# The output projections of a two-layer decoder trunk: products, operands and the norm behind them in a written order on TensorE, VectorE and ScalarE

## The chip, the cores and the metric

The kernel runs on one core of a Trainium2 chip. TensorE multiplies matrices into PSUM banks, VectorE (DVE) and ScalarE (ACT) work elementwise on SBUF and PSUM, GpSimd (POOL) works elementwise on SBUF, SyncE (SP) issues transfers. The metric is the device time of one execution in microseconds (us). A measurement of this kernel tells differences of about 0.2% from no change.

## The reference

The reference is a causal decoder trunk of two layers on one sequence of 1024 tokens with 1024 features, in float32. Layer 0 is an RMSNorm, a sparse attention (compressed blocks, selected blocks and a sliding window), a residual, an RMSNorm, a SwiGLU block (FFN) with 2816 hidden features, and a residual. Layer 1 has dilated attention over shared keys and values, with three groups of heads merged, and then the same residual, norm and FFN. What matters here is the seam between attention and FFN, in both layers: the attention's rows times the output weights are added to x, and h = rmsnorm(x) goes into x + (silu(h W_gate) * (h W_up)) W_down, with

```python
def rmsnorm(x, g):
    x32 = x.astype(jnp.float32)
    y = x32 * lax.rsqrt(jnp.mean(x32 * x32, axis=-1, keepdims=True) + RMS_EPS)
    return (y * g.astype(jnp.float32)).astype(x.dtype)
```

## The kernel before, in words

**Precision.** A float32 operand of TensorE is split into a high part `ph` (ScalarE, L884) and a low part `pl`, the rest (VectorE, or GpSimd where `Pairs` is called with it, L885). A pair costs one instruction on each of the two engines. `mm3` multiplies two pairs with three matmuls of 128x512: high by high (L203), then L204 and L205 with one low part each. The norm's operands are split in the same way by `split` (L165 on ScalarE, L166 on VectorE).

**The output projection** `out_proj` multiplies the attention's rows (tile `oT` in layer 0, `oTb` in layer 1) by the output weights (tile `ow`) and adds the result to the residual rows `xr`. The 1024x1024x1024 product is cut into 512x512 blocks and done with seven block products, in this order: B11, B21, T1, T2, B22, T3, T4. Each has four chunks (k-slices of 128), and each chunk multiplies four row tiles `t` by 512 columns: 4 x 3 = 12 matmuls a chunk, 48 a block product, 336 in all. The left operands are blocks of the attention's rows (B11, B21, B22 and T4's) or sums of blocks, built by VectorE: L1213 adds two blocks for T1, L1214 subtracts for T2, L1215 for B22, L1216 for T3. The right operands are blocks of the weights; those whose names begin with T come precombined from memory, and their low parts are made by GpSimd. Results gather in two groups of four banks, `dx0` to `dx3` and `dr0, dr1, ux, uy`. After a block product the row-adds (L1204, one for each row tile) add the four banks to `xr` on VectorE. T3 and T4 both gather in the `dx` banks, T4 going on with T3's sums, so a product of T4 may write to a bank only when T3's row-add has read it. T4 takes its row tiles one after the other over all four chunks; the others go chunk by chunk.

**The norm behind it.** Rows 0 to 3 (of eight row tiles) are complete after B22. `B.half(xr, 0, ...)` norms them: a square with a sum over the first 512 columns (ScalarE, L1011) and one over the second 512 (VectorE, L1012), a sum of the two (L1014), a root (ScalarE, L1015), a reciprocal (L1016), a scaled copy of each half (VectorE L1017, ScalarE L1018) into eight tiles `xn`. TensorE then transposes them (L990), and they are split into the FFN's operands B11 and B21. Rows 4 to 7 get the same treatment later, within the FFN.

**Order.** A list of steps is run by `staged` (L901): each step's `prep` is issued ahead of the previous step's `run`, so the first chunk of a block product is prepared one step ahead, and within a step each chunk's operands are built just ahead of its products. The norm is a step of its own ahead of T4. This is the order in which the program is written; a scheduler that goes by estimated times then places the instructions of all engines, so products of the output projection may stand between instructions of the attention, and norm instructions between operands. The pair buffers are 6 deep, those with GpSimd's low parts 4.

**The neighbours.** In the FFN, `load_up` fetches up weights (SyncE, L1267) into places of `oT` that the output projection no longer needs, and GpSimd multiplies them by the norm's gains (L1269). `dense` calls all this once per layer. The dilated attention ahead of layer 1's projection ends with the merge of its groups (matmuls L1745, products on VectorE L1746, sums on GpSimd L1747).

Of the kernel before, what the change touches and what calls it, by code (L numbers as in the profile page):

```python
# [10 lines left out]
F32 = mybir.dt.float32  # L11
F32R = mybir.dt.float32r
BF = mybir.dt.bfloat16
AF = mybir.ActivationFunctionType
# [6 lines left out]
D = 1024  # L21
# [94 lines left out]
def trunk(ctx, tc, I, out):  # L116
# [278 lines left out]
    with ExitStack() as c:  # L395
# [153 lines left out]
        next(made)  # L549
        for _ in steps:  # L550
            pass
        kc2 = blocks_tile()
# [618 lines left out]
    def out_steps(spare, pairs, tmp, blocks, right, xr):  # L1171


        held = {}
        n = len(blocks)
        S_ = [tmp(i) for i in range(n)]

        def step(left, name, group, first, where, sums=None, whole=False):
            def operands(i):
                if sums is not None:  # L1180
                    sums(i, *blocks[i])
                return pairs(left(i)), right(name, i)

            def prep():
                ready = [operands(0)]

                def run():
                    if whole:
                        ready.extend(operands(i) for i in range(1, n))
                        order = [(i, t) for t in range(4) for i in range(n)]  # L1190
                    else:
                        order = [(i, t) for i in range(n) for t in range(4)]
                    if first:
                        held[group] = [bank((f"dx{t}", spare[t])[group]) for t in range(4)]
                    banks = held[group]
                    for i, t in order:
                        if i == len(ready):
                            ready.append(operands(i))
                        a, b = ready[i]
                        mm3(banks[t], part(a, t), b, first and i == 0, i == n - 1, True)  # L1200
                        if i == n - 1:
                            r, c = where
                            xs = xr[:, 4 * r + t, c * 512:(c + 1) * 512]
                            nc.vector.tensor_add(xs, xs, banks[t])  # L1204
                return run
            return prep

        A = lambda j: lambda i: blocks[i][j]
        T = lambda i: S_[i]
        sub, add = nc.vector.tensor_sub, nc.vector.tensor_add  # L1210
        return [step(A(0), "B11", 0, True, (0, 0)),
                step(A(2), "B21", 1, True, (0, 0)),
                step(T, "T1", 1, True, (1, 1), lambda i, a11, a21, a12, a22: add(S_[i], a21, a22)),  # L1213
                step(T, "T2", 0, False, (0, 1), lambda i, a11, a21, a12, a22: sub(S_[i], S_[i], a11)),  # L1214
                step(A(2), "B22", 1, False, (0, 1), lambda i, a11, a21, a12, a22: sub(a12, a12, S_[i])),  # L1215
                step(A(1), "T3", 0, False, (1, 1), lambda i, a11, a21, a12, a22: sub(a21, a11, a21)),  # L1216
                step(A(3), "T4", 0, False, (1, 0), whole=True)]

    def out_proj(layer, pw, pp, p, xr, oT, w, x_src, norm):
        pairs, made = Pairs(pp, 6), Pairs(p, 4)  # L1220
        raw = {}
# [8 lines left out]

        def right(name, i):
            t = raw[name, i]
            return pairs(t) if name[0] == "B" else made(t, nc.gpsimd)
# [163 lines left out]
    def dense(layer, w, x_src, oT, tail, near, far):  # L1397
# [3 lines left out]
        with ExitStack() as c:  # L1401
# [4 lines left out]
            with ExitStack() as c2:  # L1406
                pw, pp, p = [pool(c2, n, near) for n in ("fow", "fop", "fo")]
                out_proj(layer, pw, pp, p, xr, oT, w, x_src, B.half(xr, 0, ("dr0", "dr1", "ux", "uy"), places(p)))
# [430 lines left out]
```

## Time and profile before

| | us |
|---|---|
| median of three runs | 2977.77 |
| lowest, highest | 2974.25, 2978.2 |
| the profiled execution's own time | 2971.67 |
| its span in the trace | 2969.9 |
| output projection, layer 0: last attention matmul, first FFN product | 724.66, 815.92 |

In rows of the profile, `PE dx L203 <- DVE nss L1016` means that a matmul of line 203 into tile dx waited, and that the last thing it waited for was VectorE's instruction of line 1016 on tile nss. A wait is put down to the engine's instruction that was counted last, so the instruction that matters can stand right behind the one named. Windows give the busy time of each engine within a stretch, the number of instructions, and the clock that TensorE was granted (1.00 is full). At full clock the products of the output projection follow each other by 0.2267 us.

### The profile page before, as it was taken

The page shows a single profiled execution, that of the slowest core. Times are in us where ns is not written, and L with a number is a line of the kernel's source. Part 1 is how long each engine was busy: PE and PEld are TensorE (multiplying, and loading weights), DVE is VectorE, ACT ScalarE, POOL GpSimd, SP SyncE. Part 2 cuts the span into 40 slices and gives each one's busy share as a digit, 9 for nine tenths or more (in the row PEclk, how much of TensorE's full clock was granted, in tenths as well). Part 3 has the DMA queues.
Part 4 walks back from the last instruction along what each step waited for, and adds up shares of the span by engine and source line. Part 5 has one row for each costly group of instructions (what it writes and reads, how often), then busy time and mean ns, then how long its engine had stood idle before and what let it go on. Part 6 is the DMA issues. An engine that isn't in the chain of part 4 may idle for free.

```text
span 2969.9 us, 44462 instructions
## 1 busy us (share of the span) xinstructions
PE 2839.8 (96%) x14734; PEld 2368.8 (80%) x14734; DVE 2398.1 (81%) x4875; ACT 1608.9 (54%) x3614; POOL 1607.7 (54%) x1718
## 2 busy tenths in 40 slices
PE   9999999999999999999999999899989999999997
PEld 8888888887777788788777788788867787887885
DVE  5553988988888888988876676699998888888887
ACT  5432888897553333333454444799965433333334
POOL 3135766764565555555557786444426655556551
PEclk9999999999999999999999999999999999999998
DMA  8678133113222222231224555966340211112112
GB/s 252 209 246 285 46 91 87 54 30 118 68 62 64 73 75 62 62 81 53 86 81 143 160 165 152 288 195 181 101 167 22 68 57 53 57 47 64 54 43 75
DMA packets 277318, 317.58 MB, mean 107 GB/s; under 512 B 19196, under 2 KB 210733, under 8 KB 277088
## 3 DMA queue, kind: packets, MB, share of 16 engines
q1 hardware_dynamic: 255344, 246.50, 27.9%
q0 software_dynamic: 21744, 68.23, 7.1%
q8 instruction: 117, 1.92, 0.3%
q14 instruction: 113, 0.93, 0.1%
HBM read 243.17 MB, written 87.20 MB: 111 GB/s over the span
## 4 chain that ended last, share of the span: by engine, by line
PE 62%; DVE 23%; ACT 6%; issue 4%; POOL 2%; DMA 2%; SPq 1%; DVEq 0%; ACTq 0%; POOLq 0%
PE ux L203 5%; PE ux L204 5%; DVE pl L885 5%; PE ux L205 5%; PE uy L203 4%; PE uy L204 4%; PE uy L205 4%; DVE xr L943 4%; PE dx L204 3%; PE dx L205 3%; PE pt L328 3%; PE dr L203 3%; PE dx L203 3%; PE mm L204 3%; PE mm L203 3%
## 5 line engine op out<-in xcount | busy, mean ns | idle before, releaser
L885 DVE TENSOR_TENSOR pl<-oT,ph 128x512 fp32r<-128x512 f32 x319 | 327.2, 1045 | 42.5 <-ACT ph L884 37.2
L884 ACT ACTIVATE ph<-oT 128x512 fp32r<-128x512 f32 x329 | 198.4, 625 | 206.8 <-PE ux L204 58.9
L328 PE MATMUL pt<-ident,P 128*128 128x128 f32 x1536 | 242.3, 275 | 10.6 <-DVE tl L166 4.9
L885 DVE TENSOR_TENSOR pl<-oTb,ph 128x512 fp32r<-128x512 f32 x233 | 222.3, 979 | 25.2 <-ACT ph L884 25.2
L166 DVE TENSOR_TENSOR tl<-pt,th 128x512 fp32r<-128x512 f32 (+1 forms) x336 | 217.4, 652 | 26.8 <-ACT th L165 25.5
L884 ACT ACTIVATE ph<-oTb 128x512 fp32r<-128x512 f32 x239 | 142.8, 625 | 170.2 <-PE ux L204 52.5
L943 DVE TENSOR_TENSOR xr<-xr,dr 128x512 f32<-128x512 f32 x320 | 204.3, 678 | 29.9 <-PE dr L205 29.9
L204 PE MATMUL dx<-pl,ph 128*128 128x512 f32 x512 | 206.3, 403 | 9.9 <-DVE pl L885 7.3
L803 POOL TENSOR_SCALAR P<-P,sm,gates 128x384 f32<-128x384 f32 (+7 forms) x256 | 182.5, 724 | 45.2 <-DVE sm L801 40.0
L165 ACT ACTIVATE th<-pt 128x512 fp32r<-128x512 f32 (+1 forms) x336 | 185.0, 564 | 37.4 <-PE pt L328 31.6
L205 PE MATMUL dx<-ph,pl 128*128 128x512 f32 x512 | 202.5, 398 | 0.3 <-DVE pl L885 0.3
L328 PEld LDWEIGHTS pt<-ident,P 128*128 128x128 f32 x1536 | 177.7, 141 | 31.4 <-DVE tl L166 5.2
L943 DVE TENSOR_TENSOR xr<-xr,dx 128x512 f32<-128x512 f32 x320 | 199.9, 676 | 2.5 <-PE dx L205 1.8
L203 PE MATMUL dx<-ph 128*128 128x512 f32 x512 | 165.6, 403 | 15.9 <-DVE nss L1016 7.9
L799 ACT ACTIVATE P<-P,m 128x384 f32<-128x384 f32 (+7 forms) x256 | 170.6, 669 | 9.0 <-DVE m L797 7.2
L1269 POOL TENSOR_TENSOR oT<-oT,gffn 128x512 f32<-128x512 f32 x92 | 107.7, 1177 | 118.8 <-DMA oT<-in_ffn_w_up_dram 96.5
L348 PE MATMUL o<-th,V 128*128 128x256 f32 x572 | 158.7, 297 | 4.5 <-DVE o L360 1.7
L349 PE MATMUL o<-tl,V 128*128 128x256 f32 x572 | 158.2, 299 | 4.7 <-DVE tl L166 1.7
L1269 POOL TENSOR_TENSOR oTb<-oTb,gffn 128x512 f32<-128x512 f32 x92 | 106.5, 1167 | 87.9 <-DMA oTb<-in_ffn_w_up_dram 79.8
L341 POOL TENSOR_SCALAR th<-traw 128x256 fp32r<-128x256 f32 x112 | 95.4, 852 | 98.2 <-ACT traw L340 33.1
L1646 ACT ACTIVATE P<-P,st 128x384 f32<-128x384 f32 (+2 forms) x256 | 139.9, 548 | 6.3 <-DVE st L1641 5.0
L203 PEld LDWEIGHTS dx<-ph 128*128 128x128 f32 x512 | 97.8, 191 | 45.4 <-ACT nss L1015 8.7
(629 smaller groups left out, 9487.8 us busy)
## 6 DMA issues: line engine op xcount, KB each, us to landing
qB<-xr POOLq DMA_DIRECT2D x96, 256.0 KB, 4.6
oT<-in_ffn_w_up_dram SPq DMA_DIRECT2D x92, 256.0 KB, 3.0
oTb<-in_ffn_w_up_dram SPq DMA_DIRECT2D x92, 256.0 KB, 3.0
Q<-qB SPq DMA_DIRECT2D x40, 512.0 KB, 6.4
wd<-in_ffn_w_down_dram SPq DMA_DIRECT2D x66, 256.0 KB, 2.6
oT<-in_b_w_q_dram SPq DMA_DIRECT2D x48, 256.0 KB, 3.4
K<-kBs SPq DMA_DIRECT2D x40, 256.0 KB, 9.6
wraw<-in_a_w_in_dram SPq DMA_DIRECT2D x18, 512.0 KB, 7.1
```

The source lines that it names most:

```text
L165: prev = nc.scalar.activation(H_, src, AF.Copy)
L166: rest = (eng or nc.vector).tensor_sub(L_, src, f32(H_))
L203: nc.tensor.matmul(ps, lh, rh, start=first, stop=False, skip_group_check=bool(shared))
L204: nc.tensor.matmul(ps, lh, rl, start=False, stop=False, skip_group_check=bool(shared))
L205: return nc.tensor.matmul(ps, ll, rh, start=False, stop=last, skip_group_check=bool(shared))
L328: nc.tensor.transpose(ps[:, i * 128:(i + 1) * 128], b, ident)
L799: nc.scalar.activation(P[:, e, :n], P[:, e, :n], AF.Exp, bias=mm[:, e:e + 1], scale=-1.0, accum_out=sm[:, e:e + 1])
L803: nc.gpsimd.tensor_scalar(P[:, e, :n], P[:, e, :n], sm[:, e:e + 1], gt(g, t, br, 2 * hp + e, 1), op0=OP.mult, op1=OP.mult)
L884: nc.scalar.activation(h, src, AF.Copy)
L885: (eng or nc.vector).tensor_sub(l, src, f32(h))
L943: nc.vector.tensor_add(xs, xs, banks[t])
L1269: nc.gpsimd.tensor_mul(v, v, gains[:, k:k + 4].unsqueeze(2).to_broadcast([128, 4, 128]))
```

## The change

In `out_proj` the list of steps is gone (`out_steps` is deleted), and the seven block products stand in a loop within `tc.manual_schedule` for TensorE, VectorE and ScalarE: what is written there keeps its order on these three engines. Instructions of other parts can still be put between them by the scheduler; GpSimd and SyncE stay with the scheduler.

- Operands are built two chunks ahead of their products; GpSimd's right operands are asked for two chunks further ahead (`right(n + 2)` in `operands(n)`). The pair buffers are 8 deep (before 6), GpSimd's 5 (before 4).
- In each chunk all three matmuls of a row tile are written together, tile by tile.
- The norm of rows 0 to 3 is written into the last two block products. While T3 runs, behind the operands of each chunk, `squares(i)` takes one square of 1024 columns on ScalarE with its sum (line 1244 of the new program) and the root (1245); `scaled(i - 1)` then takes the reciprocal (1250) and the scaled copy, on VectorE alone for odd tiles (1252, 1024 columns) and half by half on VectorE and ScalarE for even ones (1254, 1255). The sums L1014 and the squares L1012 of this half are gone. The `xn` tiles are four of 1024 columns.
- T4 runs tile by tile; the transposes into B11 come behind its first tile, those into B21 behind the third.
- In layer 0's attention one step of the output of blocks (`next(made)`) moves behind the rest of the compression's steps.

New line numbers: the left sums are 1206 to 1209, the row-adds 1236, the FFN's gain products 1310, the merge's matmuls 1786. What a name with a number means below: `nss2_` a tile's sum of squares, `ph_`/`pl_` one pair's parts, `ow_` a right block, `xn` a normed tile.

First place, ScalarE in layer 0 from the norm's roots to the last operands of T4. Before:

```order
L884 ACTIVATE ph_10912<-ow_10270 128x512
L1015 ACT_TABLE_LOAD
L1015 ACTIVATE nss2_10733<-nss2_10733,eps_69 128x1
L884 ACTIVATE ph_10920<-ow_10272 128x512
L1015 ACTIVATE nss2_10741<-nss2_10741,eps_69 128x1
L1015 ACTIVATE nss2_10749<-nss2_10749,eps_69 128x1
L1018 ACTIVATE xn10_10208<-xr_10185,nss2_10733 128x512
L1015 ACTIVATE nss2_10757<-nss2_10757,eps_69 128x1
L1018 ACTIVATE xn11_10209<-xr_10185,nss2_10741 128x512
L1018 ACTIVATE xn12_10210<-xr_10185,nss2_10749 128x512
L884 ACTIVATE ph_10928<-ow_10274 128x512
L1018 ACTIVATE xn13_10211<-xr_10185,nss2_10757 128x512
```

Now:

```order
L1244 ACTIVATE xn2_10274,nss2_10819<-xr_10185 128x1024
L1245 ACTIVATE nss2_10819<-nss2_10819,eps_69 128x1
L884 ACTIVATE ph_10836<-ow_10266 128x512
L884 ACTIVATE ph_10840<-oT_2663 128x512
L1244 ACTIVATE xn3_10275,nss2_10844<-xr_10185 128x1024
L884 ACTIVATE ph_11052<-oT_2663 128x512
L884 ACTIVATE ph_11056<-oT_2663 128x512
L884 ACTIVATE ph_11074<-oT_2663 128x512
L1245 ACTIVATE nss2_10844<-nss2_10844,eps_69 128x1
L1255 ACTIVATE xn2_10274<-xr_10185,nss2_10819 128x512
L884 ACTIVATE ph_10854<-oT_2663 128x512
L884 ACTIVATE ph_10860<-oT_2663 128x512
```

Before, right operands (`ow_`) stand between the small roots, and the squares are done earlier. Now squares of 1024 columns and roots stand between T4's operands, and three operands of the FFN (`ph_11052` to `ph_11074`) stand ahead of the last root and of chunks 26 and 27 (`ph_10854`, `ph_10860`).

Second place, VectorE at the end of T3 in layer 0, with the row-adds of T3 (`dx`). Before:

```order
L885 TENSOR_TENSOR pl_10917<-oT_2663,ph_10916 128x512
L1014 TENSOR_TENSOR nss2_10733<-nss2_10733 128x1
L1012 ISA xn13_10211,nss2_10757<-xr_10185 128x512
L1012 ISA nss2_10757 128x1
L1014 TENSOR_TENSOR nss2_10741<-nss2_10741 128x1
L885 TENSOR_TENSOR pl_10925<-oT_2663,ph_10924 128x512
L1014 TENSOR_TENSOR nss2_10749<-nss2_10749 128x1
L1016 RECIPROCAL nss2_10733<-nss2_10733 128x1
L1014 TENSOR_TENSOR nss2_10757<-nss2_10757 128x1
L1204 TENSOR_TENSOR xr_10185<-xr_10185,dx0_10296 128x512
L1016 RECIPROCAL nss2_10741<-nss2_10741 128x1
```

Now:

```order
L885 TENSOR_TENSOR pl_10816<-oT_2663,ph_10815 128x512
L1250 RECIPROCAL nss2_10793<-nss2_10793 128x1
L1252 TENSOR_SCALAR xn1_10273<-xr_10185,nss2_10793 128x1024
L885 TENSOR_TENSOR pl_10841<-oT_2663,ph_10840 128x512
L1250 RECIPROCAL nss2_10819<-nss2_10819 128x1
L1254 TENSOR_SCALAR xn2_10274<-xr_10185,nss2_10819 128x512
L1236 TENSOR_TENSOR xr_10185<-xr_10185,dx0_10294 128x512
L1236 TENSOR_TENSOR xr_10185<-xr_10185,dx1_10295 128x512
L1236 TENSOR_TENSOR xr_10185<-xr_10185,dx2_10296 128x512
L1236 TENSOR_TENSOR xr_10185<-xr_10185,dx3_10297 128x512
L1012 ISA wd2_11033,nss2_11130<-xr_10185 128x512
L1012 ISA nss2_11130 128x1
```

The four row-adds stand together now, behind the low part of chunk 25 (`pl_10841`) and the scaling of tile 2; the low part of chunk 26 comes behind them and behind an FFN square (L1012).

Third place, TensorE in the dilated attention of layer 1: L348 and L349 are the attention's, L203 to L205 with `dx` the output projection's. Before, 18 products stand within the attention, of which the first six are here:

```order
L349 MATMUL o_24564<-tl_24595,V00_23765 128x256
L203 MATMUL dx0_25032<-ph_25020,ph_25016 128x512
L204 MATMUL dx0_25032<-pl_25021,ph_25016 128x512
L205 MATMUL dx0_25032<-ph_25020,pl_25017 128x512
L203 MATMUL dx1_25033<-ph_25020,ph_25016 128x512
L204 MATMUL dx1_25033<-pl_25021,ph_25016 128x512
L205 MATMUL dx1_25033<-ph_25020,pl_25017 128x512
```

Now the first product follows the merge's last matmul:

```order
L349 MATMUL o_24776<-tl_24796,V00_23754 128x256
L1786 MATMUL pt_24834<-crow1_19744,rowsel_19747 128x512
L1786 MATMUL pt_24837<-crow1_19744,rowsel_19747 128x512
L1786 MATMUL pt_24841<-crow1_19744,rowsel_19747 128x512
L1786 MATMUL pt_24844<-crow1_19744,rowsel_19747 128x512
L203 MATMUL dx0_25019<-ph_25007,ph_25003 128x512
L204 MATMUL dx0_25019<-pl_25008,ph_25003 128x512
L205 MATMUL dx0_25019<-ph_25007,pl_25004 128x512
```

Nothing of the output projection stands within the attention any more, and the three matmuls of a row tile follow each other. The instructions of the dilated attention itself also come in another order in places, though its code is the same.

The diff, without the deleted `out_steps` (printed above) and `right`:

```diff
@@ compress, layer 0
         tok_proj(wide(wts, W[:, 1792:2048], 256, 4), 256, hT, natural, evac_v(0))
-        next(made)
         for _ in steps:
             pass
+        next(made)
@@ out_proj
-        pairs, made = Pairs(pp, 6), Pairs(p, 4)
-        raw = {}
+        pairs, made = Pairs(pp, 8), Pairs(p, 5)
+        raw, lefts, rights = {}, {}, {}
...
-        steps = out_steps(("dr0", "dr1", "ux", "uy"), pairs, lambda i: p.tile([128, 512], F32, name=f"ta{i}"), blocks,
-                          right, xr)
-        staged(steps[:6] + [norm] + steps[6:])
+        def right(n):
+            if n < 28 and steps[n // 4][1][0] == "T":
+                rights[n] = made(raw[steps[n // 4][1], n % 4], nc.gpsimd)
+
+        def operands(n):
+            right(n + 2)
+            if n < 28:
+                left, name, _, _, _, sums = steps[n // 4]
+                i = n % 4
+                if sums is not None:
+                    sums(i, *blocks[i])
+                lefts[n] = pairs(left(i))
+                if name[0] == "B":
+                    rights[n] = pairs(raw[name, i])
...
+        def squares(j):
+            ss = cst.tile([128, 2], F32, name="nss2", bufs=8)
+            rs = ss[:, 0:1]
+            nc.scalar.activation(xn[j], xr[:, j, :], AF.Square, accum_out=rs)
+            nc.scalar.activation(rs, rs, AF.Sqrt, bias=eps, scale=1.0 / D)
+            B.rs.append(rs)
+
+        def scaled(j):
+            rs = B.rs[j]
+            nc.vector.reciprocal(rs, rs)
+            if j % 2:
+                nc.vector.tensor_scalar(xn[j], xr[:, j, :], rs, None, op0=OP.mult)
+            else:
+                nc.vector.tensor_scalar(xn[j][:, lo], xr[:, j, lo], rs, None, op0=OP.mult)
+                nc.scalar.activation(xn[j][:, hi], xr[:, j, hi], AF.Copy, scale=rs)
...
+        with tc.manual_schedule(engines={E.PE, E.DVE, E.Activation}):
+            operands(0)
+            operands(1)
+            for s in range(6):
+                _, _, group, first, _, _ = steps[s]
+                if first:
+                    held[group] = [bank((f"dx{t}", ("dr0", "dr1", "ux", "uy")[t])[group]) for t in range(4)]
+                for i in range(4):
+                    for t in range(4):
+                        products(s, i, t)
+                    operands(4 * s + i + 2)
+                    if s == 5:
+                        squares(i)
+                        if i > 0:
+                            scaled(i - 1)
+                for t in range(4):
+                    to_rows(s, t)
+            operands(26)
+            scaled(3)
+            operands(27)
+            for t in range(4):
+                for i in range(4):
+                    products(6, i, t)
+                if t in (0, 2):
+                    turned(*(("B11", lo), ("B21", hi))[t // 2])
+                to_rows(6, t)
```

More of the change, by code (lines that the diff above doesn't have):

```diff
@@ L1169, in places @@
         return [[p.tile([128, 512], F32, name=f"xn{h}{j}") for j in range(4)] for h in range(2)]
[L1171 to L1217, printed above, removed]
@@ L1247, in out_proj @@
         blocks = [(oT[:, i, lo], oT[:, i, hi], oT[:, i + 4, lo], oT[:, i + 4, hi]) for i in range(4)]
-        steps = out_steps(("dr0", "dr1", "ux", "uy"), pairs, lambda i: p.tile([128, 512], F32, name=f"ta{i}"), blocks,
-                          right, xr)
-        staged(steps[:6] + [norm] + steps[6:])
+        S_ = [p.tile([128, 512], F32, name=f"ta{i}") for i in range(4)]
+        A = lambda j: lambda i: blocks[i][j]
+        T = lambda i: S_[i]
+        sub, add = nc.vector.tensor_sub, nc.vector.tensor_add
@@ new lines, in out_proj, with products, to_rows @@
+        held = {}
+        def products(s, i, t):
+            first = steps[s][3]
+            return mm3(held[steps[s][2]][t], part(lefts[4 * s + i], t), rights[4 * s + i], first and i == 0, i == 3, True)
+        def to_rows(s, t):
+            r, c = steps[s][4]
+            xs = xr[:, 4 * r + t, c * 512:(c + 1) * 512]
+            nc.vector.tensor_add(xs, xs, held[steps[s][2]][t])
+        xn = [p.tile([128, D], F32, name=f"xn{j}") for j in range(4)]
+        B.rs = []
+        def squares(j):
[4 more added lines that the diff above has]
+            B.rs.append(rs)
@@ new lines, in scaled, with turned @@
+        def scaled(j):
[6 more added lines that the diff above has]
+                nc.scalar.activation(xn[j][:, hi], xr[:, j, hi], AF.Copy, scale=rs)
+        def turned(name, cols):
+            for i, b in enumerate(("dr0", "dr1", "ux", "uy")):
+                pt = bank(b)
+                for j in range(4):
+                    nc.tensor.transpose(pt[:, j * 128:(j + 1) * 128],
+                                        xn[j][:, cols.start + i * 128:cols.start + (i + 1) * 128], ident)
+                split(*B.ops[name][i], pt)
@@ L1407, in dense @@
                 pw, pp, p = [pool(c2, n, near) for n in ("fow", "fop", "fo")]
-                out_proj(layer, pw, pp, p, xr, oT, w, x_src, B.half(xr, 0, ("dr0", "dr1", "ux", "uy"), places(p)))
+                out_proj(layer, pw, pp, p, xr, oT, w, x_src, B)
             with ExitStack() as cu:
```

13 lines of the change are left out of this document (9 added, 4 removed).

## The prediction

> **What bounds the kernel now.** I read the page first, then the waits of TensorE, the windows around the output projections, and the timelines of the engines in them. The page's first part shows TensorE busy in nearly all of the span:
>
> ```profile
> PE 2839.8 (96%) x14734; PEld 2368.8 (80%) x14734; DVE 2398.1 (81%) x4875; ACT 1608.9 (54%) x3614; POOL 1607.7 (54%) x1718
> ```
>
> The work of TensorE does not change, so the change can only win what TensorE loses, about 4% in all, in the places it touches. The waits of TensorE over the whole span (line waited for: total us, times, longest) name three of them:
>
> ```profile
> PE dx L203 <- DVE nss L1016: 7.9, 2, 4.0
> PE dx L204 <- DVE pl L885: 7.3, 2, 6.6
> ...
> PE dx L204 <- POOL pl L885: 1.7, 1, 1.7
> ```
>
> The first row is the last product of each output projection, once per layer. The 6.6 us of the second are the start of the projection of layer 1, and the third row lies in layer 1 too. A wait has a second price. These windows begin at the end of four waits (us; TensorE, weight loads, VectorE, ScalarE, GpSimd busy; the granted clock is the third number from the right):
>
> ```profile
> 799.20:804.30 5.10, 5.10 (x15) 4.08 (x16) 5.10 (x10) 4.72 (x9) 4.08 (x4) 0.53 0.02 3
> 2270.30:2275.40 5.10, 5.10 (x15) 4.08 (x16) 5.10 (x9) 4.12 (x8) 3.02 (x3) 0.52 0.02 3
> 2205.50:2210.60 5.10, 5.10 (x13) 3.99 (x14) 5.10 (x9) 1.15 (x2) 0.00 (x0) 0.53 0.79 265
> 2237.00:2242.00 5.00, 5.00 (x22) 4.16 (x23) 2.59 (x2) 1.16 (x2) 5.00 (x4) 1.00 0.06 15
> ```
>
> After the waits of 4.0, 4.0 and 6.6 us the clock is 0.52 to 0.53 for 5.1 us, which loses 5.1 x 0.47 = 2.4 us. After the wait of 1.7 us it is 1.00. So the last product of each layer costs 4.0 + 2.4 = 6.4 us, the start of layer 1 6.6 + 2.4 = 9.0, the last row 1.7: 23.5 us, 0.8% of the span.
>
> **The last product of each layer.** Why TensorE waits there, in VectorE's timeline of layer 0 (start, us, engine, line; in brackets the wait ahead):
>
> ```profile
> 795.31 0.68 DVE L885 TENSOR_TENSOR pl<-oT,ph 128x512 fp32r<-128x512 f32 x1
> 795.91 1.21 DVE L1014 TENSOR_TENSOR nss<-nss 128x1 f32<-128x1 f32 x1
> 797.04 0.15 DVE L1016 RECIPROCAL nss<-nss 128x1 f32<-128x1 f32 x1
> 797.12 1.23 DVE L1014 TENSOR_TENSOR nss<-nss 128x1 f32<-128x1 f32 x1
> 798.27 0.68 DVE L1204 TENSOR_TENSOR xr<-xr,dx 128x512 f32<-128x512 f32 x1
> ```
>
> TensorE resumes at 799.1, after the row-add L1204, for the last product accumulates in the bank which that add reads. The add stands in VectorE's order behind the norm's tiny sums L1014, at 1.2 us each although they handle 128 numbers. Those, and the squares L1012, leave VectorE with the change. Prices that I use (ns, minimum/median/maximum, from the groups that touch xr):
>
> ```profile
> L1204 DVE TENSOR_TENSOR xr<-xr,dr x12: 673/678/689, 750.3 to 2257.0; 128x512 f32<-128x512 f32 x12
> L1011 ACT ACTIVATE xn<-xr x12: 617/631/633, 751.0 to 2225.9; 128x512 f32<-128x512 f32 x12
> L1011 ACT ACTIVATION_READ_ACCUMULATOR xn<-xr x12: 185/187/188, 751.5 to 2226.4; 128x1 f32 x12
> L1012 DVE CUSTOM_DVE_ANT_0 xn<-xr x12: 677/686/1780, 787.0 to 2264.7; 128x512 f32<-128x512 f32 x12
> L1018 ACT ACTIVATE xn<-xr,nss x12: 706/722/726, 797.4 to 2273.2; 128x512 f32<-128x512 f32 x12
> L1017 DVE TENSOR_SCALAR xn<-xr,nss x12: 466/544/1380, 798.9 to 2274.9; 128x512 f32<-128x512 f32 x12
> ```
>
> Three more from ScalarE's timeline, the table load, the square root and one high part of an operand:
>
> ```profile
> 790.67 1.28 ACT L1015 ACT_TABLE_LOAD   x1
> 793.65 0.29 ACT L1015 ACTIVATE nss<-nss,eps 128x1 f32<-128x1 f32 x1 [1.70 <-DVE nss L1014]
> 793.85 0.62 ACT L884 ACTIVATE ph<-ow 128x512 fp32r<-128x512 f32 x1
> ```
>
> And the low parts of the right operands, on GpSimd and on VectorE:
>
> ```profile
> L885 POOL TENSOR_TENSOR pl<-ow,ph x32: 1277/1684/2031, 733.9 to 2272.8; 128x512 fp32r<-128x512 f32 x32
> L885 DVE TENSOR_TENSOR pl<-ow,ph x24: 675/687/1779, 728.1 to 2250.4; 128x512 fp32r<-128x512 f32 x24
> ```
>
> In a row on one engine such pieces follow each other about 0.1 us closer than they last (795.31 to 795.91 above), so I count 0.53 and 0.60. Count from the end of the fifth product on TensorE. VectorE's four row-adds end 1.0 later, the sum of chunk 22 at 1.7, its high part on ScalarE at 2.3. From there ScalarE's new order is one chain: a square of 1024 (631 + 530 + about 90 of the accumulator = 1.25), table load 1.28, root 0.2, two high parts 1.05, square 1.25, root 0.2, the scaled half of tile 0 0.65, two high parts, square 1.25, root 0.2, two high parts: the last, chunk 25, at 11.75. VectorE then has, in its order, the low part of chunk 25 (12.35), a reciprocal and a scaled half (12.95), and only then the row-add of T3 (13.55). TensorE ends T3 at 48 x 0.2267 = 10.9 (0.2267 being the spacing of products at full clock; 48 are one product of blocks), so it waits **2.7**. It does six products of chunks 24 and 25 to 14.95. ScalarE meanwhile: square 3 (13.0), three FFN parts (14.6), root, scaled half, chunk 26's high part (16.0); VectorE: the other adds 15.35, an FFN square 16.0, chunk 26's low part 16.6: TensorE waits **1.7**. Then reciprocal, scaled(3) over 1024 (0.9), low part of 27 at 18.2: **0.9** more. In sum 5.3 against 6.4: -1.1 us if the clock holds, +1.3 if it falls as before. But the pieces of VectorE in that chain (low parts 25, 26 and 27 and a sum) cost 1.78 in place of 0.68 where GpSimd works beside them, and GpSimd has four right parts, two gain products and four FFN parts of 1.28 to 1.7 in these 14 us. All four hit, and the clock too: 5.3 + 4.4 + 2.4 - 6.4 = +5.7. Range -1.1 to +5.7. I take **+0.8** per layer, some collisions and no more than part of the clock's fall, since each single wait is nearer to the 1.7 that kept it than to the 4.0 that lost it: **+1.6** for both.
>
> [...]
>
> **The start of layer 1.** The windows of two stretches in which only products of the output projection run, between those of the attention, and the timeline's row where TensorE comes back after its wait:
>
> ```profile
> 2178.25:2182.36 4.11, 4.11 (x20) 3.36 (x19) 2.80 (x7) 4.04 (x14) 0.00 (x0) 1.00 0.00 0
> 2193.69:2198.60 4.91, 4.91 (x23) 3.94 (x21) 4.88 (x7) 4.55 (x10) 4.03 (x3) 1.00 0.00 1
> ```
>
> ```profile
> 2205.48 0.79 PE L204 MATMUL dx<-pl,ph 128*128 128x512 f32 x1 [6.60 <-DVE pl L885]
> ```
>
> So 9.0 us of products, 18 and 22 of the 336 (the counts take in neighbours at the edges), are done before that wait. In the new order none is, and this work is added behind the attention. But VectorE's path to the first product is shorter. Before it was:
>
> ```profile
> 2195.61 4.21 DVE L1213 TENSOR_TENSOR ta<-oTb 128x512 f32<-128x512 f32 x3
> 2199.75 1.74 DVE L1216 TENSOR_TENSOR oTb<-oTb 128x512 f32<-128x512 f32 x1
> 2201.41 1.74 DVE L885 TENSOR_TENSOR pl<-oTb,ph 128x512 fp32r<-128x512 f32 x1
> ```
>
> In the new order the low parts of chunk 0 follow the attention directly, and the sums come four chunks later. Break-even: at 2205.48 there were 296 products left; a first L204 with one product done has 335 left, 39 x 0.2267 = 8.8 us more, so it must come by 2196.7, if the clock falls in both. VectorE ends the attention at 2195.61, and two low parts bring the first L204 to 2197.0: +0.3. But the attention loses the preparation of six operands, in these windows of VectorE (L885) and of ScalarE (L884):
>
> ```profile
> 2158.00:2171.00 13.00, 4.01 (x6) 0.00 (x0) 1.00 0.97 344
> ```
>
> ```profile
> 2158.00:2171.00 13.00, 3.51 (x6) 1.00 0.97 344
> ```
>
> If all of VectorE's 4.0 us moved its end, it is -3.7. The tail is a chain of small waits, so I take a third of the 4.0, 0.3 - 1.3 = **-1.0**. On the other side the attention's instructions stand in another order now, and I allow +3.
>
> **The rest.** The 1.7 us of the third wait go, since GpSimd's parts are asked for four chunks ahead in place of one:
>
> ```profile
> 2236.98 0.50 PE L204 MATMUL dx<-pl,ph 128*128 128x512 f32 x1 [1.72 <-POOL pl L885]
> ```
>
> GpSimd does no less, so 0 to **-1.7**, and I take all of it. The start of layer 0 waits for the attention's last rows and one high part:
>
> ```profile
> 726.99 1.20 PE L203 MATMUL dx<-ph 128*128 128x512 f32 x4 [2.04 <-ACT ph L884]
> ```
>
> That is the same in the new order, 0; the sums gone from VectorE's front there are set off by TensorE taking L204 right behind the first L203. The loads of the up weights go out later, when their place in oT is free; GpSimd multiplies them beside the products, 0 to +2 per layer. The compress step moved in layer 0's attention lies where TensorE is the bound, 0, and the reordered dilated attention 0, plus or minus 3.
>
> Sum: 1.6 - 1.0 - 1.7 = **-1.1 us**: 2971.67 to 2970.6 for the profiled execution. That run was 6.1 below the median of the three runs; on the median it is 2977.77 - 1.1 = **2976.7**. About 0.2%, 6 us, is what a measurement of this kernel tells from no change.
>
> **The rivals.** A, the likeliest, no difference to be seen: the wait at L1204 becomes three shorter ones behind ScalarE. Own range 2971 to 2982.
>
> B, faster: waits under about 3 us keep the clock, at all three places, and the attention's tail gives VectorE's 4.0 us back. Then -1.1 x 2 in the norm, -3.7 and -2.4 at layer 1's start, -1.7: -10.0, **2967.8**. For it: the clock row at 2237 behind 1.7 us. Against it: GpSimd (fifth of the busy times) works for 7.4 of the 10 us before, so collisions are likely:
>
> ```profile
> 790.00:800.00 10.00, 6.03 (x25) 4.75 (x24) 10.00 (x19) 5.19 (x11) 7.41 (x6) 0.86 0.10 26
> ```
>
> [...]
>
> C, slower: GpSimd sets the pace of the norm. Its right parts and FFN parts hold VectorE's pieces at 1.78 all along, and ScalarE's third FFN part, which stands ahead of the last root and of chunks 26 and 27, waits for GpSimd's part of chunk 27. That is +5.7 in each layer; with -1.7 and -1.0, +8.7, **2986.5**. It decides as soon as two of VectorE's four pieces are held and one wait reaches 4 us. For it: 1.74 twice in the rows at 2199.75 and 2201.41, and 1.2 at L1014. Against it: the pair at 795.31 took 0.68.
>
> D: only the attention's new order shows, plus or minus 3, which lies within A.
>
> **How the numbers follow.** A 0.38 (D with it), B and its milder forms 0.33, C and its milder forms, or 3 us lost at the tail, 0.29. The range goes from B with 5 us of the rest, **2963**, to C with the up weights' 2, **2989**. Faster 0.33, same 0.38, slower 0.29.
>
> **What would show it.** Right: no wait of TensorE for nss; in T4 waits of 1 to 3 us for L1236 and for low parts of VectorE, in sum 5 to 8 us per layer; the clock over 0.8 there; no output product inside the dilated attention, and the first L204 behind it within 2194 to 2198 when shifted to the clock of before. Wrong: T4 without waits, or waits of over 9 us there; the attention itself longer or shorter by over 4 us; a new wait at the FFN's first products for gain products on GpSimd.

## The result and the profile after

| | before | after |
|---|---|---|
| median, us | 2976.0 (4 runs) | 3007.9 (4 runs) |
| ratio, 95% interval | | 1.0108 [1.0091, 1.0126] |
| profiled execution, span | 2969.9 | 3006.5 |
| layer 0: last attention matmul to first FFN product | 91.3 | 104.7 |
| dilated attention: first to last matmul of L347 to L349 | 304.4 | 308.1 |
| layer 1: last attention matmul to first FFN product | 96.0 | 109.5 |
| from there to the end | 682.8 | 683.3 |

The change is 1.1% slower, and lies outside the forecast's range. The rows are worked out from the starts of two rows each in TensorE's timeline (the FFN's first product is the first L203 that reads B11 or B21). Of the 36.6 us between the two profiled executions 26.9 lie in the two output projections, 13.4 and 13.5. The dilated attention is 3.7 longer, although 4.1 us of output products no longer stand in it; in the runs below it takes between 303.6 and 311.0, and in e13, whose output projection is written as here, 304.2, so the 3.7 is not put down to the change. The other 6.0 are spread over the rest (2.9 ahead of the first projection, 2.7 between the first FFN product and the dilated attention, 0.4 at the end); the time up to the last matmul of layer 0's attention differs by 8 us among the runs below, so nothing is read into these.

TensorE's waits of layer 0 from 733 to 828 us, which answer to the rows of L1016 and L885 before:

```profile
PE dx L203 <- ACT ph L884: 5.9, 2, 5.6
PE dx L205 <- DVE pl L885: 2.9, 3, 2.0
PE dr L204 <- DVE pl L885: 2.3, 2, 2.1
PE dr L203 <- ACT ph L884: 0.2, 1, 0.2
```

The norm's row is gone, as foreseen. In its place TensorE waits 5.6 us ahead of T4's first product and 2.0 within T4, and 2.1 in B22 (`dr`), where it had not waited. The clock behind these waits, third number from the right:

```profile
809.30:822.10 12.80, 10.58 (x32) 8.04 (x33) 9.83 (x13) 5.88 (x10) 9.04 (x7) 0.51 0.08 22
786.86:790.98 4.12, 4.12 (x12) 3.22 (x13) 2.94 (x3) 1.44 (x3) 1.93 (x2) 0.61 0.22 64
```

T4's first 12.8 us run at half clock. TensorE works in 10.6 of them and waits in the rest, so 10.6 x 0.49 = 5.2 us are lost to the clock (before 2.4), and 1.6 at B22's end, with a clock of 0.61. Take the last attention matmul and the first FFN product as two marks. In layer 0 the idle time of TensorE between them goes from 6.7 to 13.3 us. With 4.4 us more lost to the clock and 0.9 for eight transposes that now come ahead of the second mark, that makes 11.9 of the 13.4; the other 1.5 are not accounted for.

VectorE at the end of B22, in time (the bracket is its own pause):

```profile
786.73 0.68 DVE L1209 TENSOR_TENSOR oT<-oT 128x512 f32<-128x512 f32 x1
788.19 0.69 DVE L885 TENSOR_TENSOR pl<-oT,ph 128x512 fp32r<-128x512 f32 x1 [0.78 <-ACT ph L884]
788.80 1.78 DVE L1209 TENSOR_TENSOR oT<-oT 128x512 f32<-128x512 f32 x1
791.36 0.69 DVE L885 TENSOR_TENSOR pl<-oT,ph 128x512 fp32r<-128x512 f32 x1 [0.78 <-ACT ph L884]
791.97 1.28 DVE L1236 TENSOR_TENSOR xr<-xr,dr 128x512 f32<-128x512 f32 x2
...
794.36 0.88 DVE L1209 TENSOR_TENSOR oT<-oT 128x512 f32<-128x512 f32 x1
```

Each sum (L1209) is followed by a pause of 0.78 us: ScalarE must make the high part of the sum before VectorE can make its low part, and nothing else may stand between. So B22, whose right operands are VectorE's too, takes it per chunk a sum, the pause and two low parts, 3 x 0.60 + 0.78 = 2.6 us, and 4 x 0.60 of row-adds: 12.8 us, and more with each piece of 1.78, against 10.9 of TensorE. VectorE falls behind. T3 begins at 790.98; the row-adds that were counted to end 1.0 later end at 794.4.

ScalarE's chain and what VectorE does at its end, one after the other:

```profile
795.35 0.63 ACT L884 ACTIVATE ph<-oT 128x512 fp32r<-128x512 f32 x1 [3.50 <-DVE oT L1209]
795.89 1.05 ACT L1244 ACTIVATE xn<-xr 128x1024 f32<-128x1024 f32 x1
796.84 0.19 ACT L1244 ACTIVATION_READ_ACCUMULATOR xn<-xr 128x1 f32 x1
797.04 1.28 ACT L1245 ACT_TABLE_LOAD   x1
798.34 0.29 ACT L1245 ACTIVATE nss<-nss,eps 128x1 f32<-128x1 f32 x1
...
804.75 0.61 ACT L884 ACTIVATE ph<-oT 128x512 fp32r<-128x512 f32 x1
```

```profile
805.40 1.49 DVE L885 TENSOR_TENSOR pl<-oT,ph 128x512 fp32r<-128x512 f32 x1 [0.18 <-ACT ph L884]
806.82 0.15 DVE L1250 RECIPROCAL nss<-nss 128x1 f32<-128x1 f32 x1
807.00 1.55 DVE L1254 TENSOR_SCALAR xn<-xr,nss 128x512 f32<-128x512 f32 x1
808.48 2.47 DVE L1236 TENSOR_TENSOR xr<-xr,dx 128x512 f32<-128x512 f32 x4
```

The row-adds of T3 (808.48) come behind the low part of chunk 25 and a scaling, both held at 1.5 us, and T4 begins at 809.30. GpSimd works beside both:

```profile
804.92 1.42 POOL L885 TENSOR_TENSOR pl<-ow,ph 128x512 fp32r<-128x512 f32 x1 [1.12 <-ACT ph L884]
807.00 5.68 POOL L885 TENSOR_TENSOR pl<-oT,ph 128x512 fp32r<-128x512 f32 x4 [0.66 <-ACT ph L884]
```

### The profile page after: what moved, and what is told of

Read it like the earlier page. It is cut to its first block, busy times and chain, and to the rows that moved or that the text cites. A ratio compares the mean times of both kernels' runs of the same rounds, so it can differ in the third digit from the quotient of the medians.

```text
span 3006.5 us, 44398 instructions
## 1 busy us (share of the span) xinstructions
PE 2861.5 (95%) x14734; PEld 2384.3 (79%) x14734; DVE 2395.2 (80%) x4851; ACT 1613.0 (54%) x3610; POOL 1605.0 (53%) x1718
## 5 line engine op out<-in xcount | busy, mean ns | idle before, releaser
L885 DVE TENSOR_TENSOR pl<-oT,ph 128x512 fp32r<-128x512 f32 x319 | 327.3, 1044 | 53.8 <-ACT ph L884 47.9
L885 DVE TENSOR_TENSOR pl<-oTb,ph 128x512 fp32r<-128x512 f32 x233 | 225.5, 992 | 32.8 <-ACT ph L884 32.8
L204 PE MATMUL dx<-pl,ph 128*128 128x512 f32 x512 | 206.6, 404 | 4.4 <-DVE pl L885 3.3
L205 PE MATMUL dx<-ph,pl 128*128 128x512 f32 x512 | 203.7, 400 | 6.5 <-DVE pl L885 6.5
L203 PE MATMUL dx<-ph 128*128 128x512 f32 x512 | 173.7, 407 | 20.4 <-ACT ph L884 16.9
L349 PE MATMUL o<-tl,V 128*128 128x256 f32 x572 | 160.0, 302 | 5.1 <-POOL tl L342 2.0
L348 PE MATMUL o<-th,V 128*128 128x256 f32 x572 | 160.7, 300 | 4.2 <-DVE oTb L360 2.1
L1310 POOL TENSOR_TENSOR oTb<-oTb,gffn 128x512 f32<-128x512 f32 x92 | 108.0, 1182 | 96.0 <-DMA oTb<-in_ffn_w_up_dram 87.4
L203 PEld LDWEIGHTS dx<-ph 128*128 128x128 f32 x512 | 99.1, 194 | 50.6 <-issue 13.3
```

The lines of the kernel that those rows point to most:

```text
L203: nc.tensor.matmul(ps, lh, rh, start=first, stop=False, skip_group_check=bool(shared))
L204: nc.tensor.matmul(ps, lh, rl, start=False, stop=False, skip_group_check=bool(shared))
L205: return nc.tensor.matmul(ps, ll, rh, start=False, stop=last, skip_group_check=bool(shared))
L885: (eng or nc.vector).tensor_sub(l, src, f32(h))
L1310: nc.gpsimd.tensor_mul(v, v, gains[:, k:k + 4].unsqueeze(2).to_broadcast([128, 4, 128]))
```

## The experiments

There were three theories at first. N: the norm's pieces among the last operands. P: the order itself, which makes VectorE and ScalarE wait for each other at every sum. O: the parts around the projections. All runs in one table: the time between the two marks in each layer and the median, in us; the ratio is to before. The whole times hold more than the projections: the profiled executions also differ by up to 8 us ahead of the first mark and by up to 10 between the layers, so the columns of the layers say more about the edits.

| run | layer 0 | layer 1 | median | ratio, 95% interval |
|---|---|---|---|---|
| before | 91.3 | 96.0 | 2970.6 to 2976.0 | |
| the change | 104.7 | 109.5 | 3007.9 | 1.0108 [1.0091, 1.0126] |
| e1 norm late | 97.9 | 102.1 | 2985.3 | 1.0033 [1.0022, 1.0044] |
| e2 scalings late | 101.3 | 106.2 | 2993.1 | 1.0059 [1.0042, 1.0076] |
| e3 sums early | 96.6 | 102.6 | 2987.9 | 1.0050 [1.0035, 1.0065] |
| e4 scheduler | 85.9 | 90.7 | 2963.1 | 0.9955 [0.9939, 0.9972] |
| e5 order on TensorE, VectorE | 106.1 | 110.7 | 3000.1 | 1.0084 [1.0056, 1.0111] |
| e6 order on TensorE, ScalarE | 95.9 | 97.0 | 2975.2 | 1.0001 [0.9990, 1.0012] |
| e7 sums early, norm late | 92.4 | 96.2 | 2981.7 | 1.0019 [1.0006, 1.0032] |
| e8 order on TensorE | 91.6 | 98.4 | 2970.9 | 0.9993 [0.9980, 1.0005] |
| e9 order on VectorE | 99.8 | 102.0 | 2989.9 | 1.0062 [1.0041, 1.0084] |
| e10 no gain products | 101.5 | 107.4 | 2979.4 | 1.0026 [1.0012, 1.0040] |
| e11 scheduler, old compress step | 87.4 | 90.7 | 2963.4 | 0.9964 [0.9951, 0.9977] |
| e12 order up to T1 | 89.6 | 92.8 | 2963.1 | 0.9972 [0.9959, 0.9985] |
| e13 FFN parts off GpSimd | 106.0 | 110.7 | 3009.6 | 1.0116 [1.0087, 1.0146] |
| e14 e13 and sums early | 100.4 | 103.5 | 2997.3 | 1.0080 [1.0056, 1.0104] |

**e1, the norm behind the operands.**

```diff
                     operands(4 * s + i + 2)
-                    if s == 5:
-                        squares(i)
-                        if i > 0:
-                            scaled(i - 1)
...
             operands(26)
-            scaled(3)
             operands(27)
+            for j in range(4):
+                squares(j)
+                scaled(j)
...
-                if t in (0, 2):
-                    turned(*(("B11", lo), ("B21", hi))[t // 2])
+                if t >= 2:
+                    turned(*(("B11", lo), ("B21", hi))[t - 2])
```

> The change with the norm's squares and scalings taken out of T3 and written behind the operands of T4 (chunks 26 and 27); the transposes come behind the third and fourth row tile of T4. Theory N (the norm's pieces, written among the last operands of T3 and T4 on ScalarE and VectorE, hold T3's row-adds and the last operands): the waits of TensorE in T4, 8.8 us per layer now, fall under 2 us and the half clock there goes, some 13 us per layer, so about 2982 us. Theory P (the written order makes VectorE and ScalarE wait for each other at every sum, high part and low part, so operands run late whether the norm is there or not): half of that stays, about 2995. Theory O (most of the loss lies in the attention and projections around, whose order came out otherwise): no more than 5 us less, 3003.

22.5 us of the 32 come back, as N had it for the whole time. But 8.1 of them lie ahead of the first mark, where e1 changes nothing. Between the marks it is 14.2 of 26.9, about half, as P had it. The 5.6 us wait goes; what stays is 2.1 in B22 and, new, 2.7 at the transposes for the scaled rows (L1252).

**e2, only the scalings behind the operands.**

```diff
                     if s == 5:
                         squares(i)
-                        if i > 0:
-                            scaled(i - 1)
...
             operands(26)
-            scaled(3)
             operands(27)
+            for j in range(4):
+                scaled(j)
...
-                if t in (0, 2):
-                    turned(*(("B11", lo), ("B21", hi))[t // 2])
+                if t in (1, 2):
+                    turned(*(("B11", lo), ("B21", hi))[t - 1])
```

> The change with the squares where they are, among T3's operands, and only the reciprocals and scalings behind chunk 27's operands; transposes behind the second and third row tile. Theory N: it splits the blame. The row-adds lose the scaling ahead of them (1.7 us), but chunk 25's low part still waits for three squares and the table load on ScalarE, so the first wait in T4 goes from 5.6 to about 3.9 and the two later ones to under 1, 4 to 6 us per layer, about 2997. If the scaling on VectorE were the whole of it, about 2985. Theory P: about 3000. Theory O: 3005.

14.8 us come back, nearer to 2997 than to 2985, but only 6.7 of them between the marks. T4's first wait is 2.9 (3.9 had been said), and 2.3 and 0.7 follow within T4 (under 1 had been said of the two).

**e3, each sum one chunk earlier.**

```diff
         def operands(n):
             right(n + 2)
+            if n < 27 and steps[(n + 1) // 4][5] is not None:
+                i = (n + 1) % 4
+                steps[(n + 1) // 4][5](i, *blocks[i])
...
-                if sums is not None:
-                    sums(i, *blocks[i])
```

> The change with each left sum written one chunk earlier, so that VectorE does the sum of the next chunk while ScalarE makes the high part of this one. Theory P: VectorE's pauses of 0.78 us at each sum go, the wait of 2.1 us in B22 and its half clock too, and the norm's chain starts some 2.5 us earlier: 8 to 10 us per layer, about 2990. Theory N: the wait in T4 becomes 2 to 3 us shorter per layer, about 3001. Theory O: 3006.

20 us come back, more than N and P had said; between the marks it is 15.0, and 5.2 lie ahead of the first. The wait in B22 is gone and T3 runs without one. But T4's first wait is still 5.1 us. Here the chain started in time (the first square 2.6 behind T3's first product, at 779.85; counted: 2.3) and its last high part ended 11.8 behind it (counted: 11.75). What is left shows on VectorE behind it, in the rows ahead of T4:

```profile
792.12 1.75 DVE L885 TENSOR_TENSOR pl<-oT,ph 128x512 fp32r<-128x512 f32 x1
793.79 0.15 DVE L1251 RECIPROCAL nss<-nss 128x1 f32<-128x1 f32 x1
793.98 1.30 DVE L1255 TENSOR_SCALAR xn<-xr,nss 128x512 f32<-128x512 f32 x1
795.20 2.47 DVE L1237 TENSOR_TENSOR xr<-xr,dx 128x512 f32<-128x512 f32 x4
```

1.75 and 1.30 where 0.68 and 0.47 were the times without GpSimd; its low parts (788.67 to 799.40) run beside both. So with VectorE's pauses the waits in B22 and T3 go, but of T4's 5.6 us only 0.5.

**e4, the same program, placed by the scheduler.**

```diff
-        with tc.manual_schedule(engines={E.PE, E.DVE, E.Activation}):
+        with ExitStack():
```

> The change with the same program text, but without the written order: the scheduler places the instructions of all engines again. If the order as written is at fault (N or P), the scheduler starts operands and row-adds when they can run and products of layer 1 stand within the attention again: 2975 to 2985. If the new pieces themselves (squares of 1024 on ScalarE, two chunks ahead, bigger buffers) are at fault, 3000 or more.

This is the run that decides. Without the written order the change is faster than before by 0.45%, at 2963.1, and so 12 us under the range expected. Of the 42.3 us between its profiled execution and the change's 37.6 lie between the marks. Between 785 and 812 us, all of T3 and T4 of layer 0, TensorE never stops and keeps its clock:

```profile
785.00:812.00 27.00, 27.00 (x137) 22.77 (x136) 23.05 (x45) 23.05 (x48) 16.36 (x12) 1.00 0.04 11
```

ScalarE in that run shows why: the left operands are made two at a time as buffers come free, ahead of the squares, and the squares run behind one another in a gap:

```profile
784.68 1.16 ACT L884 ACTIVATE ph<-oT 128x512 fp32r<-128x512 f32 x2 [1.57 <-PE uy L204]
786.67 1.06 ACT L1244 ACTIVATE xn<-xr 128x1024 f32<-128x1024 f32 x1 [0.83 <-DVE xr L1236]
787.64 0.18 ACT L1244 ACTIVATION_READ_ACCUMULATOR xn<-xr 128x1 f32 x1
787.73 1.14 ACT L884 ACTIVATE ph<-oT 128x512 fp32r<-128x512 f32 x2
788.89 1.28 ACT L1245 ACT_TABLE_LOAD   x1
```

They wait for TensorE, not for VectorE's sums as in the written order (3.50 <- DVE oT L1209): the sums of T3 (L1209) had been done at 732.3 to 737.2, some 50 us before. Products of layer 1's projection do not stand within the attention here either, against the expectation; the first L204 comes 8.9 us behind the attention (6.6 in the change). So the new pieces are sound, and the order is what costs 45 us.

**e5, e6, e8, e9, on which engine.** The line is the same in each, with fewer engines:

```diff
-        with tc.manual_schedule(engines={E.PE, E.DVE, E.Activation}):
+        with tc.manual_schedule(engines={E.PE, E.DVE}):          # e5
+        with tc.manual_schedule(engines={E.PE, E.Activation}):   # e6
+        with tc.manual_schedule(engines={E.PE}):                 # e8
+        with tc.manual_schedule(engines={E.DVE}):                # e9
```

> The change with the written order on TensorE and VectorE only; ScalarE goes back to the scheduler. Theory V (VectorE's order is at fault: each sum right ahead of its low part, T3's row-adds behind a low part and a scaling): the 2.1 us in B22 stay and the row-adds still wait for the scaling of tile 2, so most of the loss stays, 2992 to 3005. Theory S (ScalarE's order is at fault: the high parts of chunks 24 to 27 stand behind squares, roots and FFN parts): these go, 2965 to 2978.

> The change with the written order on TensorE and ScalarE only; VectorE goes back to the scheduler. Theory V: sums run ahead and row-adds are taken when their bank is ready, so the loss goes, 2965 to 2978. Theory S: chunks 26 and 27 still stand behind the squares on ScalarE, T4 waits 4 to 6 us per layer, 2985 to 2998.

> The change with the written order on TensorE only. Theories V and S both say that TensorE's order is harmless: within 5 us of the run where the scheduler places all, 2958 to 2968. A rival, T (TensorE's order, three matmuls tile by tile and T4's tiles with the transposes at fixed places, makes it wait): 2980 or more.

> The change with the written order on VectorE only; TensorE and ScalarE go back to the scheduler. If VectorE's order alone carries the loss (theory V), 2990 to 3005, with waits of 4 us and more for T4's first product. If it needs TensorE's fixed order beside it (the scheduler can move TensorE's other work into the gaps), 2965 to 2980.

Against e4's 2963.1: TensorE alone +8 us, TensorE and ScalarE +12, VectorE alone +27, TensorE and VectorE +37, all three +45. Between the marks of both layers it is 13.4, 16.3, 25.2, 40.2 and 37.6. V holds, and the order on VectorE alone is over half of the loss; ScalarE's adds nothing between the marks to that of TensorE and VectorE. e9 ends just under V's range, and its first wait in T4 is 3.3 us in layer 0 and 4.6 in layer 1, where 4 and more had been said. TensorE's own order is not quite harmless, against V and S: e8 misses its range by 3 us, with waits of 0.4 to 1.9 for row-adds (L1236). With VectorE fixed, TensorE's waits (layer 0, 733 to 828) stay also when ScalarE is free, as in e5:

```profile
PE dx L205 <- DVE pl L885: 4.4, 2, 2.4
PE dx L203 <- ACT ph L884: 4.2, 1, 4.2
PE dr L204 <- DVE pl L885: 2.4, 2, 2.2
PE dx L203 <- DVE xr L1236: 0.8, 1, 0.8
```

**e7, sums early and norm late, in the written order.** It has the edits of e1 and e3.

> The change with its written order on all three engines, with each sum one chunk earlier and the norm behind T4's operands. The two edits alone gave 20 and 22.5 us less than the change. If they take away different waits (pauses at the sums; norm ahead of operands) they add up to nearly the time of the scheduler's order, 2968 to 2975. If both only shorten the same chain into T4, 2982 to 2986.

Between the marks the two nearly add up: e1 saves 6.8 and 7.4, e3 8.1 and 6.9, both 12.3 and 13.3, so for the most part they take away different waits. In the whole time, 2981.7, they do not (26 where 42 would be the sum). But of those 42, 8.1 and 5.2 lie ahead of the first mark, where neither has an edit. Behind the second mark of layer 1 this run is 4.9 longer than the change, and why is not settled.

**e10, without GpSimd's gain products.**

```diff
-            k = q % 2 * 4
-            nc.gpsimd.tensor_mul(v, v, gains[:, k:k + 4].unsqueeze(2).to_broadcast([128, 4, 128]))
```

> The change without GpSimd's products of the up weights with the norm's gains, so this run leaves out that multiplication in all of the FFN. It asks how much of the waits in T3 and T4 comes from VectorE's pieces being held by GpSimd's. Where those products are gone, collisions are fewer but do not end, since the low parts of right operands and the FFN's parts stay. If collisions are the main price in T4 (my forecast's case C): the first wait there falls from 5.6 to about 4, the wait in B22 to under 1. If the order is (theory V): both change by less than 1 us. The whole time says little here, since the FFN has less to do.

The outcome is split. The waits in layer 0 from 733 to 828 are now

```profile
PE dx L203 <- ACT ph L884: 7.2, 3, 5.6
PE dx L205 <- DVE pl L885: 3.5, 3, 2.6
PE dr L204 <- DVE pl L885: 0.5, 2, 0.3
```

The 2.1 us in B22 go, so collisions with these products, on top of the pauses, put a wait there. But 1.2 us of waiting appear in T3, T4's 5.6 stays and 0.6 come to its later wait: in sum 11.4 us where the change has 11.3. VectorE is no less late without these products: it ends the row-adds 6.0 us behind T3's first product (783.88), where it was 3.4 in the change.

**e13, e14, the FFN's first low parts on VectorE.** e14 has e3's edit too.

```diff
-                               eng=nc.gpsimd if j < 3 else None)
+                               eng=nc.gpsimd if 0 < j < 3 else None)
```

> The change with the low parts of the FFN's first block of products on VectorE in place of GpSimd, so that GpSimd has no FFN parts beside T4's operands. If GpSimd holds VectorE's low part of chunk 25 and the scaling ahead of T3's row-adds (case C of the forecast), these go from 1.5 us each to 0.7 and 0.5, and the first wait of T4 from 5.6 to about 3.8. If the late start of the chain is the whole of it, 5.6 stays. The whole time may even grow, for VectorE gets the FFN's parts: 2995 to 3012.

> Both together: sums one chunk earlier (no late start) and no FFN parts on GpSimd (fewer collisions). If late start and collisions are all that my count of the chain missed, the first wait of T4 is what I had counted, 2.7 us (2.3 to 3.3). If it stays over 4, the count itself is wrong and the cause is still open. Whole time 2975 to 2988.

In e13 the scaling falls from 1.55 to 0.49, the low part of chunk 25 stays at 1.50, for GpSimd's low part of a right operand runs beside it, and the wait falls from 5.6 to 4.5 (3.8 had been said). In e14 it is 4.4, not 2.7, and the whole time 2997 lies above the range expected. VectorE ahead of T4:

```profile
797.41 1.57 DVE L1253 TENSOR_SCALAR xn<-xr,nss 128x1024 f32<-128x1024 f32 x1
798.91 1.75 DVE L885 TENSOR_TENSOR pl<-oT,ph 128x512 fp32r<-128x512 f32 x1
800.59 0.15 DVE L1251 RECIPROCAL nss<-nss 128x1 f32<-128x1 f32 x1
800.77 0.48 DVE L1255 TENSOR_SCALAR xn<-xr,nss 128x512 f32<-128x512 f32 x1
801.17 2.47 DVE L1237 TENSOR_TENSOR xr<-xr,dx 128x512 f32<-128x512 f32 x4
```

ScalarE's chain ended at 798.4, so VectorE came 0.5 late to the low part, still in a scaling of 1.57, and was then held 1.07 longer (1.75 for 0.68): GpSimd's three low parts of right operands stand there from 795.5 to 800.1. That is 1.6 of the 1.7 us that are over the count. The expectation had said that over 4 the count is wrong and the cause open. By these rows the count of ScalarE's chain holds and the collisions are more than the FFN's; this is read from the trace. No run took away all collisions, so that 2.7 would then be left is not shown.

**e11, e12, towards a faster version.** e11 is e4 with the compression's step at its old place; e12 takes the written order for the first three block products only.

```diff
+        next(made)                     # e11, with ExitStack() as in e4
         for _ in steps:
             pass
-        next(made)
...
         with tc.manual_schedule(engines={E.PE, E.DVE, E.Activation}):   # e12
             operands(0)
             operands(1)
-            for s in range(6):
...
+            for s in range(3):
+                product(s)
+        for s in range(3, 6):
+            product(s)
...
```

> The scheduler's order with the step of layer 0's compression put back where it was, so of the change only the new output projection is left. The move lies where TensorE is never idle, so I expect no difference from the run with the scheduler's order, 2958 to 2968. If the gain of that run came from the move, this is like before, 2970 to 2978.

> The written order for the first three block products (B11, B21, T1), where its trace has only the waits at the start, and the scheduler's order from T2 on. Theory V says that the written order does harm only where sums, row-adds and the norm meet, from B22 on: the start of layer 1 is then 1.6 us shorter than with the scheduler and the rest like it, 2955 to 2965. If the written part changes how the scheduler places what follows, 2965 to 2980.

The moved step is worth nothing (2963.4 and 2963.1). e12 starts layer 1 with a wait of 3.3 us in place of e4's 4.9, but a wait of 2.2 us stands in layer 0 (765.68) that e4 does not have. Between the marks it takes 3.7 and 2.1 us longer than e4, so its even time comes from elsewhere. All three beat both kernels, by 0.3 to 0.45% of before; the simplest is e4.

## Why the prediction was wrong

The forecast was no difference to be seen, with +0.8 us a layer for the norm; +13.4 and +13.5 came. The places of the loss behind the norm were foreseen, not its size, and part of its cause not at all.

- **The step that failed first** is "VectorE's four row-adds end 1.0 later, the sum of chunk 22 at 1.7, its high part at 2.3". It took VectorE to be in time at the end of B22. They came at 3.4, 4.3 and 5.0, for VectorE had pauses of 0.78 us at each sum and 12.8 us of work and pauses in a block product of 10.9. I had read the order only where it moved row-adds and operands, and not that it binds a sum to its own low part. e3 shows it: with the sums one chunk earlier the wait in B22 goes and the chain begins nearly when I had counted. In T4's first wait VectorE's pieces (below) weigh more, for e3 still has 5.1 us of it.
- **ScalarE's chain** was right: counted 9.45 from chunk 22's high part to chunk 25's, measured 9.4 (795.98 to 805.36), 1.28 of it the table load again, with the root 0.02 behind it (798.34).
- **VectorE's pieces behind it** were counted at 1.8 and took 3.7 (805.40 to 809.1). The prediction had this as collisions, up to 4.4 per layer, but took only "some". This is the term that was too small for T4's first wait: 1.9 us in the change and 2.6 in e3 over the count. Right ahead of T3's row-adds in layer 0 the longest low part or scaling took 1.50 to 1.75 us in the change, e3, e10, e13 and e14. In e4 a scaling took 1.33 too, and TensorE did not wait for it.
- **The waits in T4** were 5.6, then 0.2 and 2.0; counted were 2.7, then 1.7 and 0.9. The later two come out near in sum (2.2 and 2.6), but by luck: TensorE ran at half clock between them, and VectorE's pieces were held at 1.75 (811.48) and 1.86 (813.34). In sum the three are 7.8, within the 5 to 8 that I had named as a sign of being right; the clock of 0.51 is not.
- **The clock** was to cost at most 2.4 us a layer, and I took a part of that. In layer 0 it cost 5.2 in T4 and 1.6 in B22, so the bound of +5.7 a layer was too low. I had gone by two lengths, the 1.7 us that kept it and the 4.0 that lost it, but my own row at 726.99 is a wait of 2.04. One of 0.67 follows it, and then 3.4 us of half clock:

```profile
728.95:732.36 3.41, 3.41 (x8) 2.64 (x9) 3.41 (x7) 0.24 (x2) 0.00 (x0) 0.50 1.01 381
```

  So short waits were no ground for counting only a part. In T4 of layer 0 the slow stretch lasted 13.7 us (808.26 to 821.92), and the second and third wait fall into it. Whether they prolonged it is not shown: in layer 1, with waits of 5.6 and 2.7, the clock was full again for 3.4 us between two slow stretches:

```profile
2296.48:2303.30 6.82, 3.49 (x8) 2.48 (x8) 6.79 (x10) 5.67 (x13) 6.06 (x5) 0.50 0.00 1
2303.30:2306.72 3.42, 1.17 (x4) 0.48 (x3) 3.38 (x4) 0.65 (x1) 2.84 (x2) 1.00 0.00 0
2306.72:2313.54 6.82, 6.10 (x22) 5.48 (x23) 3.96 (x7) 3.00 (x5) 2.83 (x3) 0.50 0.15 41
```

- **B22's wait** of 2.1 us was in no term, and neither was 1.0 us of waits in T3 (0.29 at 799.73, 0.68 at 801.14).
- **Layer 1's start** was said to gain 1.0. From the attention's last matmul to the first L204 there are 6.6 us (2213.72 to 2220.34), before 14.45 with 8.8 us of products done: 1.0 lost. The attention itself did not become shorter without the six operands; it is 3.7 longer. With 303.6 us in e12 and 307.4 in e4 it differs as much among runs that keep the new pieces, and why, the runs do not tell.
- **Right were** the norm's wait gone, the third wait gone, no loss in the FFN of layer 1 (682.8 and 683.3), and nothing from the compression's step, as far as e4 against e11 tells.
- **The rivals.** C was nearest, with GpSimd's collisions as its mechanism, but at +8.7 us for 32; that ScalarE's third FFN part would wait for GpSimd does not show (three parts in 1.65 us at 806.31, without a pause). B's premise, an estimate between the 1.7 us that kept the clock and the 4.0 that lost it, failed: the first wait was 5.6, and B22's 2.1, under B's 3, had a clock of 0.61 behind it. The case that I had not set up was that the order as a whole is the cost, though the pieces in it gain: e4 against the change, 45 us.

## What to carry to other kernels

Before fixing an order by hand, add up for each engine and each stage the work and the pauses that the order itself makes, and compare with the stage's bound: a sum, its high part and its low part written in a row turn two engines into one chain (here with a pause of 0.78 us at each sum). This case speaks for fixing the order on as few engines as possible, and last on the one with the least slack: VectorE's order alone was 27 of 45 us. A run of the same pieces without the written order is the first experiment, for it tells the pieces from the order.

## What the runs showed of the hardware

In these runs it does not hang on a wait's length alone whether it costs clock. The wait in B22 was 2.07 us in layer 0 of the change, with a clock of 0.61 behind it (row above), and 2.18 in layer 1, with 1.00 behind it (2277.48 to 2282.13). In layer 0 of e2 it was 2.3 us and of e1 2.1, with 0.65 and 1.00 behind it:

```profile
784.60:789.00 4.40, 4.40 (x13) 3.51 (x14) 2.93 (x3) 1.72 (x4) 2.07 (x2) 0.65 0.20 60
```

```profile
779.98:784.00 4.02, 4.02 (x18) 3.33 (x19) 2.95 (x3) 1.33 (x3) 1.87 (x2) 1.00 0.22 65
```

And a wait of 2.9 us ahead of T4 in e2 had a clock of 1.00 over the next 4.3 us:

```profile
804.16:808.50 4.34, 2.06 (x9) 1.39 (x9) 4.34 (x7) 2.75 (x6) 4.34 (x4) 1.00 0.01 4
```

Of these five waits between 2 and 3 us two have a slower clock behind them and three do not, the longest among the three; what decides it, no run shows. In the traces of before and of the change the stretches of half clock, but for the last of each trace, lasted 3.41 us 19 times, 6.83 ten times and 13.65 once (808.26 to 821.92 in the change).

The other fact is that a scaling with a single tensor operand (L1254) was held beside GpSimd like the subtractions of two tensors that make low parts. The scaling took 1.55 us beside it (807.00 in the change) and 0.49 where GpSimd paused (805.07 in e13), a low part 1.75 (815.12 in the change) and 0.69 (796.01). The row-adds, which read PSUM, lasted 0.66 to 0.69 each in the traces of before and of the change, also beside GpSimd (808.48 above).
